# A fourth projection chunk begun at the layer boundary, with its PSUM tile shared with the LayerNorm's mean

## The chip, the cores and the metric

The kernel runs on one core of one Trainium2 chip. The metric is the device time of one execution in microseconds (us); of several runs the median is given. The profile is one execution of the same program taken by the hardware profiler.

Engine names in the profile: PE is TensorE (matrix products), PEld its weight loads, DVE is VectorE, ACT is ScalarE, POOL is GpSimd, SP issues most transfers. SBUF is the on-chip working memory, PSUM the memory into which TensorE writes.

## The reference: what is computed

Two trunk layers run over 640 tokens (128 context tokens and 512 latent tokens) with 1024 features. Cut to what matters here, one layer is:

```python
h = x * (1 + scale) + shift                     # scale, shift from the conditioning
z = h @ w_in + b_in                             # one wide projection, cut into a_q, a_ff, a_fb, ...
...
mixed = einsum('btnd,btnd->btd', gates, proj) @ w_out
y = layer_norm(ALPHA * x + gate * mixed, ln_g, ln_b)   # over the 1024 features of a token
```

The `y` of the first layer is the `x` of the second, so between the layers the kernel must finish the projection by `w_out`, take mean and variance of every token, normalise, form the next layer's `h`, and begin the next `h @ w_in`. Everything is float32; a product is made of three products of a high and a low part in a reduced format (high by high, high by low, low by high).

## The kernel before: tiles, stages and the order of the work

**Layout.** Activations lie with features on the 128 partitions and the 640 tokens along the free axis, as eight tiles of 128 features each. [...]

**Chunks of the projection.** `w_in` is cut into chunks of 128 output columns, named by their use (a_q 0, a_i 0, a_ff 0, d_x 0 and so on). One chunk is one weight tile of 128 by 8 by 128. `take_w` (L163) loads it from memory into a `wraw` tile (three of them), copies it to a high part on ScalarE (L160) and takes the low part on VectorE (L161). High and low parts normally lie in the tiles `whi` and `wlo`, two of each; with `own="s"` they take two of the five large `s` tiles instead. `zmm` (L211) does one chunk for one half: eight steps over the features of h, three products each, accumulated in PSUM (L217).

**PSUM.** It is handed out as two tiles `g` of 512 columns and three tiles `mx` of 1024 columns, and that is all of it. A tile comes free when its last reader is done.

**Who orders the work.** The code is written as one program, and a scheduler of the language turns it into one queue for each engine, in which instructions stay in order: what comes earlier in the program goes first among what is ready by the scheduler's own model of time. It also places all waits between engines. Tiles of a kind (`t`, `e`, `mx`, ...) are handed out in turn.

**Between the layers** (`out_phase`, L1136). For each half, eight chunks of the projection by `w_out` run (L1071), each followed by transposes and statistics of its tokens (L1096, L1098). Then, per half, `out_norm` (L1100) works: it joins the statistics into mean and variance (L1106), takes the inverse root of the variance in small VectorE operations (`rsqrt`, L183), and spreads mean and root over all partitions by transposes on TensorE into one `mx` tile: the mean into columns from 0, the root into columns from 512 (L1112). Then for each of the eight feature tiles: subtract the mean (L1115, VectorE), multiply by the root (L1116, VectorE), form the high part of the next h (L1121, ScalarE) and its full value (L1127 on VectorE, or L1123 on POOL for the first half) in an `e` tile (four of them), take the low part (L1128, VectorE), and keep the scaled y for the next layer's sum (L1129, then a store on SP's queue, L1130).

The norm of the first half runs beside the `w_out` products of the second half. For the norm of the second half there is nothing left of layer 0, so `zopen` (L220) and `zstep` (L232) begin three chunks of the next layer, a_q, a_i and a_g (`FIRST`, L1309): first all their products of the first half, then, after each feature tile of the second half, the three products of that tile for each chunk. The first of the three accumulates in the two `g` tiles, the other two in one `mx` tile each, and the third's weights lie in `s` tiles. The third `mx` tile holds mean and root. The same `zopen` is used at the start of the program (L1186) with the three chunks of layer 0.

In the next layer, `hg_z` (L464) asks for a_q, a_i, a_g and then a_ff; `zchunk` (L237) takes a chunk that was begun early from `self.pre` and only evicts it from PSUM. The chunk after a_ff is d_x.

Of the kernel before, what the change touches and what calls it, by code (L numbers as in the profile page):

```python
# [13 lines left out]
ALU = mybir.AluOpType  # L14
# [3 lines left out]
L = 2  # L18
# [13 lines left out]
def _chunk_cols():  # L32
    names, cols = [], []

    def add(nm, c, i):
        names.append((nm, i))
        cols.append(c)

    def std(nm, i):
        add(nm, np.arange(_OFF[nm] + 128 * i, _OFF[nm] + 128 * i + 128), i)  # L40

    for nm in ("a_q", "a_ff", "a_fb", "a_i", "a_g", "b_q", "b_k", "b_v", "b_g"):
        for i in range(4):
            std(nm, i)
    std("c_qd", 0)
    std("c_qd", 1)
    std("c_kvd", 0)
    k0 = _OFF["c_kpe"]
    add("c_kpe", np.concatenate([np.arange(k0, k0 + 64)] * 2), 0)
    for nm in ("c_g", "d_b", "d_c", "d_x", "d_g"):  # L50
        for i in range(4):
            std(nm, i)
    for i in range(32):
        std("merge", i)
    return {n: i for i, n in enumerate(names)}, np.stack(cols)


CC, COLS = _chunk_cols()
# [29 lines left out]
class Build:  # L88
# [131 lines left out]
    def zopen(self, l, items, own):  # L220

        for nm, i in items:
            n = len(self.pre)
            w = self.take_w(self.I["win"][l, CC[nm, i]], own=own if n == 2 else None)
            if n == 0:
                ps = [self.gps() for _ in range(2)]
            else:
                x = self.mx()
                ps = [x[:, 0:512], x[:, 512:1024]]
            self.pre[nm, i] = w, ps  # L230
# [869 lines left out]
    def out_norm(self, l, p):  # L1100
        nc = self.nc
        a, e = HALVES[p]
        j0, nj, n = a // 128, (e - a) // 128, e - a
        mv = self.sm([128, nj, 2])
        for j in range(nj):
            nc.vector.bn_aggr(mv[:, j, :], self.st[:, j0 + j])  # L1106
        r = self.sm([128, nj])
        self.rsqrt(r, mv[:, :, 1], nj, 1.0, EPS)
        ps = self.mx()
        for src, o in ((mv[:, :, 0], 0), (r, 512)):  # L1110
            for j in range(nj):
                nc.tensor.transpose(ps[:, o + j * 128:o + (j + 1) * 128], src[:, j:j + 1].to_broadcast([128, 128]), self.ident)  # L1112
        for c in range(8):
            y = self.y[c][:, a:e]
            nc.vector.tensor_tensor(y, y, ps[:, 0:n], ALU.subtract)  # L1115
            nc.vector.tensor_tensor(y, y, ps[:, 512:512 + n], ALU.mult)  # L1116
            f = self.e()[:, :n]
            if l + 1 < L:
                for o, x, j in ((0, 128, 0), (128, n, 1)) if p == 0 else ((0, n, 1),):
                    A, B = self.hA[:, c, j:j + 1], self.hB[:, c, j:j + 1]  # L1120
                    nc.scalar.activation(self.h_hi[:, c, a + o:a + x], y[:, o:x], AF.Identity, bias=B, scale=A)  # L1121
                    if p == 0 and F_POOL:
                        nc.gpsimd.tensor_scalar(f[:, o:x], y[:, o:x], A, B, ALU.mult, ALU.add)  # L1123
                    elif p == 1 and F_ACT:
                        nc.scalar.activation(f[:, o:x], y[:, o:x], AF.Identity, bias=B, scale=A)
                    else:
                        nc.vector.tensor_scalar(f[:, o:x], y[:, o:x], A, B, ALU.mult, ALU.add)  # L1127
                nc.vector.tensor_tensor(self.h_lo[:, c, a:e], f, self.h_hi[:, c, a:e].bitcast(F32), ALU.subtract)  # L1128
                nc.scalar.activation(y, y, AF.Identity, bias=self.ag[:, 1, c:c + 1], scale=self.ag[:, 0, c:c + 1])  # L1129
                nc.sync.dma_start(self.ax1[c, :, a:e], y)  # L1130
            else:
                nc.scalar.activation(f, y, AF.Identity, bias=self.vec("lnb", l * 8 + c), scale=self.vec("lng", l * 8 + c))
                nc.sync.dma_start(self.O["yT"][:, c, a:e], f)
            yield c

    def out_phase(self, l):  # L1136
        self.y = [None] * 8
        self.st = self.cp.tile([128, 5, 8, 6], F32, name="st")

        keep = self.bp.tile([128, 5, 8, 128], F32R, name="m")  # L1140
        wk = lambda: self.s([128, 8, 128], F32R)
        own = {2: (keep[:, 0], keep[:, 1]), 3: (keep[:, 2], keep[:, 3]), 4: (keep[:, 4], wk()), 5: (wk(), wk())}
        w = {}
        for p, order in enumerate((range(8), range(7, -1, -1))):
            for n, c in enumerate(order):
                if p == 0 or c < 2:
                    w[c] = self.take_w(self.I["wout"][l, c], own.get(c))
                self.out_chunk(l, c, p, w[c])
                if n:
                    self.out_stats(order[n - 1], p)  # L1150
                if p and n == 1:
                    if l + 1 < L:
                        self.alloc_h()
                    norm = self.out_norm(l, 0)
                if p and n:
                    next(norm, None)
            self.out_stats(order[7], p)
        for _ in norm:
            pass
        if l + 1 < L:  # L1160
            self.zopen(l + 1, FIRST, "s")
            self.zstep((0,), range(8))
            for c in self.out_norm(l, 1):
                self.zstep((1,), (c,))
        else:
            for _ in self.out_norm(l, 1):
                pass
# [141 lines left out]
FIRST = (("a_q", 0), ("a_i", 0), ("a_g", 0))  # L1309
# [139 lines left out]
```

## Time and profile before

| | us |
|---|---|
| median of 3 runs | 2128.25 (2124.88 to 2129.24) |
| the profiled execution | 2125.51 |
| its span, first to last instruction | 2123.4 |
| TensorE busy | 2069.1 |
| VectorE busy | 1366.4 |
| ScalarE busy | 878.8 |
| GpSimd busy | 181.7 |

How to read the profile's lines: in the timeline a line has the start in us from the span's start, the duration in us, the engine, the line of the kernel, the operation, output and inputs by the program's names, sizes, and how many instructions were merged into the line. Behind them, in brackets, stands how long the engine had been idle and what ended that. A PE line's duration includes the time until its result is out, so that the lines of neighbouring products overlap; the spacing of the starts is the time that one takes in a row. In the table of windows, each row gives a stretch, its length, the busy time of PE, PEld, DVE, ACT and POOL with the number of instructions, the granted TensorE clock (1.00 is full), the busy share of the transfer engines and the GB/s moved.

### The profile page before, as it was taken

What the parts mean: (1) busy time and instruction counts of PE and PEld (TensorE: products, weight loads), DVE (VectorE), ACT (ScalarE), POOL (GpSimd) and SP (SyncE); (2) the same over time, 40 slices, a digit from 0 to 9 for tenths busy, and PEclk for the clock granted to TensorE, in tenths of its full rate; (3) what the DMA queues carried; (4) which work ended last, traced back from release to release, by engine and by line L of the source; (5) the groups of instructions that cost most, each with busy time, mean ns of one, the idle gap of its engine ahead of it and who ended that gap; (6) DMA issues with size and microseconds to landing.
All of it is one profiled execution on the core that took longest, in us unless ns stands there. A gap on an engine that the chain in (4) does not pass through costs nothing.

```text
span 2123.4 us, 36900 instructions
## 1 busy us (share of the span) xinstructions
PE 2069.1 (97%) x15114; PEld 2012.1 (95%) x15114; DVE 1366.4 (64%) x2653; ACT 878.8 (41%) x1564; POOL 181.7 (9%) x156
## 2 busy tenths in 40 slices
PE   7999999998999999999999999999999999999997
PEld 4999999997999999999989999999999999999997
DVE  6677676568676567734587776874665546775456
ACT  4333335333445466523353332343343346663332
POOL 0000000121111022200010000020000002231000
PEclk9999999999999999999999999999999999999998
DMA  7222223343334221222432212233222212112241
GB/s 284 74 73 63 66 64 101 115 154 129 125 122 148 69 63 58 66 74 80 141 118 70 71 56 74 61 131 126 85 67 63 67 58 78 60 59 65 75 164 50
DMA packets 79848, 194.64 MB, mean 92 GB/s; under 512 B 9152, under 2 KB 22208, under 8 KB 79680
## 3 DMA queue, kind: packets, MB, share of 16 engines
q1 hardware_dynamic: 76656, 186.10, 27.1%
q10 hardware_dynamic: 3024, 6.20, 0.9%
q8 instruction: 118, 1.93, 0.4%
q14 instruction: 50, 0.41, 0.1%
HBM read 184.73 MB, written 7.54 MB: 91 GB/s over the span
## 4 chain that ended last, share of the span: by engine, by line
PE 87%; DVE 8%; ACT 2%; issue 1%; DMA 1%; POOL 0%; ACTq 0%; SPq 0%; DVEq 0%; POOLq 0%
PE g L217 56%; PE g L208 14%; PE mx L790 2%; PE mx L1005 2%; PE mx L546 2%; PE mx L828 1%; DVE wlo L161 1%; PE mx L208 1%; PE mx L606 1%; PE mx L972 1%; DVE t L161 1%; PE mx L217 1%; PE mx L804 1%; PE mx L583 1%; DVE t L405 1%
## 5 line engine op out<-in xcount | busy, mean ns | idle before, releaser
L217 PE MATMUL g<-h_hi,whi 128*128 128x256 f32 (+1 forms) x2880 | 906.1, 315 | 18.5 <-DVE e L1058 7.4
L217 PE MATMUL g<-h_lo,whi 128*128 128x256 f32 (+1 forms) x2880 | 893.2, 310 | 0.8 <-DVE h_lo L431 0.3
L217 PE MATMUL g<-h_hi,wlo 128*128 128x256 f32 (+1 forms) x2880 | 892.1, 310 | 0.7 <-DVE wlo L161 0.7
L217 PEld LDWEIGHTS g<-h_hi,whi 128*128 128x128 f32 x2880 | 547.9, 190 | 27.1 <-DVE e L1058 8.5
L217 PEld LDWEIGHTS g<-h_lo,whi 128*128 128x128 f32 x2880 | 548.5, 190 | 3.6 <-DVE h_lo L431 1.8
L217 PEld LDWEIGHTS g<-h_hi,wlo 128*128 128x128 f32 x2880 | 548.1, 190 | 1.0 <-DVE wlo L161 1.0
L161 DVE TENSOR_TENSOR wlo<-wraw,whi 128x1024 fp32r<-128x1024 f32 (+1 forms) x258 | 285.7, 1108 | 280.5 <-ACT whi L160 278.5
L160 ACT CAST whi<-wraw 128x1024 fp32r<-128x1024 f32 (+1 forms) x258 | 242.5, 940 | 449.0 <-PE g L217 237.8
L208 PE MATMUL g<-t,whi 128*128 128x256 f32 (+1 forms) x1280 | 283.5, 311 | 0.9 <-ACT e L1043 0.9
L208 PEld LDWEIGHTS g<-t,whi 128*128 128x128 f32 x1280 | 214.2, 189 | 2.7 <-ACT e L1043 1.6
L208 PE MATMUL g<-t,wlo 128*128 128x384 f32 (+1 forms) x640 | 197.8, 309 | 0.0
L407 POOL TENSOR_TENSOR t<-t 128x512 f32<-128x512 f32 x56 | 82.4, 1472 | 1015.8 <-ACT t L406 686.8
L928 POOL TENSOR_SCALAR u<-u,sm 128x320 f32<-128x320 f32 (+2 forms) x80 | 89.9, 1135 | 543.3 <-DVE sm L926 510.5
L208 PEld LDWEIGHTS g<-t,wlo 128*128 128x128 f32 x640 | 121.1, 189 | 0.0
L1043 ACT ACTIVATE e<-g,hbin 128x384 f32<-128x384 f32 (+1 forms) x128 | 66.8, 523 | 105.0 <-PE g L217 102.3
L260 ACT ACTIVATE e<-g,hbin 128x384 f32<-128x384 f32 x76 | 39.9, 525 | 104.0 <-PE g L217 86.7
L261 DVE TENSOR_SCALAR e<-g,vecs 128x384 f32<-128x384 f32 x76 | 41.3, 544 | 51.4 <-ACT e L260 51.1
L476 DVE RECIPROCAL s<-e 128x384 f32<-128x384 f32 (+1 forms) x32 | 68.8, 2149 | 0.7
L405 DVE SCALAR_TENSOR_TENSOR t<-t,cf 128x512 f32<-128x512 f32 x56 | 52.7, 940 | 15.5 <-DMA t<-in_wada 15.4
L853 ACT ACTIVATE t<-mx,sm,rq 128x640 f32<-128x640 f32 (+1 forms) x40 | 31.9, 798 | 63.2 <-DVE sm L850 54.1
L535 ACT COPY t<-s 128x640 f32<-128x640 f32 x56 | 43.4, 779 | 30.3 <-DVE s L560 30.3
L1058 DVE SCALAR_TENSOR_TENSOR e<-e,g 128x384 f32<-128x384 f32 x96 | 46.3, 483 | 13.5 <-PE g L208 12.9
(290 smaller groups left out, 2653.4 us busy)
## 6 DMA issues: line engine op xcount, KB each, us to landing
wraw<-in_win SPq DMA_DIRECT2D x184, 512.0 KB, 3.6
t<-in_wada SPq DMA_DIRECT2D x128, 256.0 KB, 4.3
wraw<-in_wbr SPq DMA_DIRECT2D x64, 256.0 KB, 2.6
wraw<-in_wout SPq DMA_DIRECT2D x20, 512.0 KB, 4.4
s<-in_wada SPq DMA_DIRECT2D x16, 512.0 KB, 6.6
s<-in_nabias SPq DMA_DIRECT2D x8, 640.0 KB, 4.9
m<-in_xT SPq DMA_DIRECT2D x8, 320.0 KB, 7.4
t<-in_xT ACTq DMA_DIRECT2D x8, 320.0 KB, 5.5
```

The source lines that it names most:

```text
L160: nc.scalar.copy(hi, raw)
L161: nc.vector.tensor_tensor(lo, raw, hi.bitcast(F32), ALU.subtract)
L208: nc.tensor.matmul(o, wsl(a, k), xsl(b, k, i), start=(k == 0 and p == 0), stop=(k == nk - 1 and p == 2))
L217: nc.tensor.matmul(ps[:, :e - a], at(u, k), v[:, k, a:e], start=(k == 0 and i == 0), stop=(k == 7 and i == 2))
L405: nc.vector.scalar_tensor_tensor(acc[0], raw[0], c[0], acc[0], ALU.mult, ALU.add)
L407: nc.gpsimd.tensor_tensor(acc[1], acc[1], raw[1], ALU.add)
L476: nc.vector.reciprocal(g, r)
L535: nc.scalar.copy(km.rearrange("p (n u b) -> p n u b", u=2, b=B), ap_of(RK, 0, [[2 * B, np_], [T + B, 2], [1, B]]))
L546: nc.tensor.matmul(ps[r, j * 64:(j + 1) * 64], km[:, o:o + 64], x, start=True, stop=True)
L928: NORM(nc).tensor_scalar(p[e], p[e], sums[:, e:e + 1], None, ALU.mult)
L1043: self.zchunk(l, "merge", n * 8 + c, lambda ps, p, sl: nc.scalar.activation(th[p], ps, AF.Tanh, bias=hb, scale=0.5))
L1058: nc.vector.scalar_tensor_tensor(th[p], th[p], 1.0, ps, ALU.add, ALU.mult)
```

## The change

A fourth chunk, a_ff 0 (the forget gate of the first head), is begun between the layers as well. No PSUM tile is left for it, so it shares one with the norm of the second half:

- It takes the third `mx` tile, called `x3`. Its first half accumulates in columns 512 to 895, its second half in columns 256 to 511. Its weights take two more `s` tiles.
- The norm of the second half spreads its inverse root into columns 0 to 255 of `x3`; ScalarE copies it to an `e` tile in SBUF; then the mean is spread into the same columns 0 to 255 and stays there. The multiplication reads the root from SBUF, the subtraction reads the mean from PSUM.
- The norm of the first half, the norms of the last layer and the start of the program stay as they were.

```diff
@@ zopen
-            w = self.take_w(self.I["win"][l, CC[nm, i]], own=own if n == 2 else None)
+            w = self.take_w(self.I["win"][l, CC[nm, i]], own=own if n >= 2 else None)
             if n == 0:
                 ps = [self.gps() for _ in range(2)]
+            elif n == 3:
+                self.x3 = self.mx()
+                ps = [self.x3[:, 512:1024], self.x3[:, 256:512]]
             else:
                 x = self.mx()
                 ps = [x[:, 0:512], x[:, 512:1024]]
@@ out_norm
-        ps = self.mx()
-        for src, o in ((mv[:, :, 0], 0), (r, 512)):
+        if p and l + 1 < L:
+            ps = self.x3
+            mean, root = ps[:, 0:n], self.e()[:, :n]
+            places = ((r, 0), (mv[:, :, 0], 0))
+        else:
+            ps = self.mx()
+            mean, root = ps[:, 0:n], ps[:, 512:512 + n]
+            places = ((mv[:, :, 0], 0), (r, 512))
+        for src, o in places:
             for j in range(nj):
                 nc.tensor.transpose(ps[:, o + j * 128:o + (j + 1) * 128], src[:, j:j + 1].to_broadcast([128, 128]), self.ident)
+            if src is r and o == 0:
+                nc.scalar.copy(root, ps[:, 0:n])
         for c in range(8):
             y = self.y[c][:, a:e]
-            nc.vector.tensor_tensor(y, y, ps[:, 0:n], ALU.subtract)
-            nc.vector.tensor_tensor(y, y, ps[:, 512:512 + n], ALU.mult)
+            nc.vector.tensor_tensor(y, y, mean, ALU.subtract)
+            nc.vector.tensor_tensor(y, y, root, ALU.mult)
@@ out_phase
-            self.zopen(l + 1, FIRST, "s")
+            self.zopen(l + 1, FIRST + (("a_ff", 0),), "s")
             self.zstep((0,), range(8))
             for c in self.out_norm(l, 1):
                 self.zstep((1,), (c,))
```

## The prediction

> **What bounds the kernel now.** I read the page first (busy shares, chain), then the timeline of each engine where the two layers meet, then the waits.
>
> ```profile
> span 2123.4 us, 36900 instructions
> ...
> PE 2069.1 (97%) x15114; PEld 2012.1 (95%) x15114; DVE 1366.4 (64%) x2653; ACT 878.8 (41%) x1564; POOL 181.7 (9%) x156
> ...
> PE 87%; DVE 8%; ACT 2%; issue 1%; DMA 1%; POOL 0%; ACTq 0%; SPq 0%; DVEq 0%; POOLq 0%
> ```
>
> TensorE is busy for 97% of the span and carries 87% of the chain, so time can only be won where it stands idle. The change touches one such place, the norm of the second half between the layers. TensorE there (start, duration, line):
>
> ```profile
> 1093.13 0.60 PE L1112 MATMUL mx<-ident,sm 128*128 128x128 f32 x4
> 1095.33 0.39 PE L217 MATMUL g<-h_hi,whi 128*128 128x256 f32 x1 [1.60 <-ACT h_hi L1121]
> ...
> 1096.02 0.39 PE L217 MATMUL g<-h_lo,whi 128*128 128x256 f32 x1
> 1096.24 0.28 PE L217 MATMUL g<-h_hi,wlo 128*128 128x256 f32 x1
> 1096.36 0.28 PE L217 MATMUL mx<-h_lo,whi 128*128 128x256 f32 x1
> ...
> 1105.88 0.28 PE L217 MATMUL mx<-h_hi,s 128*128 128x256 f32 x1
> 1106.46 0.44 PE L217 MATMUL g<-h_hi,whi 128*128 128x384 f32 x1 [0.31 <-ACT whi L160]
> ...
> 1107.72 0.44 PE L217 MATMUL g<-h_hi,wlo 128*128 128x384 f32 x1 [0.65 <-DVE wlo L161]
> ...
> 1111.67 0.28 PE L217 MATMUL g<-h_hi,whi 128*128 128x256 f32 x1
> ...
> 1114.54 0.34 PE L217 MATMUL g<-h_hi,whi 128*128 128x384 f32 x1
> ```
>
> A 256-column product takes a slot of 0.12 us (1096.24 to 1096.36). From 1095.33 to 1106.00 (the last one's start plus its slot) run three chunks times eight steps times three products, 72 x 0.12 = 8.64 us of work in 10.67 us, so 2.03 us are lost in the loop, after 1.60 us of waiting for the first h_hi. After the loop 0.31 and 0.65 us go to the weights of the next chunk, which is a_ff. VectorE and ScalarE in the same stretch:
>
> ```profile
> 1087.41 0.16 DVE L195 SCALAR_TENSOR_TENSOR sm<-sm 128x2 f32<-128x2 f32 x1
> 1093.76 0.42 DVE L1115 TENSOR_TENSOR t<-t,mx 128x256 f32<-128x256 f32 x1 [6.20 <-PE mx L1112]
> 1094.22 0.42 DVE L1116 TENSOR_TENSOR t<-t,mx 128x256 f32<-128x256 f32 x1
> ...
> 1095.55 0.42 DVE L1128 TENSOR_TENSOR h_lo<-e,h_hi 128x256 fp32r<-128x256 f32 x1
> ...
> 1104.46 0.42 DVE L1128 TENSOR_TENSOR h_lo<-e,h_hi 128x256 fp32r<-128x256 f32 x1 [0.23 <-ACT h_hi L1121]
> ```
> ```profile
> 1094.68 0.60 ACT L1121 ACTIVATE h_hi<-t,hB,hA 128x256 fp32r<-128x256 f32 x1 [8.29 <-DVE t L1116]
> ...
> 1103.84 0.59 ACT L1121 ACTIVATE h_hi<-t,hB,hA 128x256 fp32r<-128x256 f32 x1
> ...
> 1107.26 0.47 ACT L260 ACTIVATE e<-g,hbin 128x256 f32<-128x256 f32 x1
> ```
>
> VectorE sets the loop's pace: four operations a step, eight steps from 1093.76 to 1104.88, 1.39 us a step against 9 x 0.12 = 1.08 us of TensorE. It runs ahead: it subtracts the mean of step c+1 while TensorE multiplies step c. That running ahead is what the change puts at stake.
>
> **How finely a wait on a PSUM tile is placed.** After the change the mean (columns 0 to 255 of x3) and the second half of a_ff (columns 256 to 511) lie in one tile. The trace shows what such neighbours do to each other:
>
> ```profile
> 1725.58 0.81 DVE L760 TENSOR_TENSOR s<-mx,s 128x640 fp32r<-128x640 f32 x1
> 1726.43 0.27 ACT L762 COPY u<-mx 128x128 f32<-128x128 f32 x1 [1.46 <-DVE s L760]
> ```
> ```profile
> 1728.26 0.38 PE L766 MATMUL mx<-u 128*128 128x128 f32 x2
> ...
> 1728.48 1.28 PE L768 MATMUL mx<-u,t 128*128 128x128 f32 x10
> 1729.80 0.27 ACT L770 COPY u<-mx 128x128 f32<-128x128 f32 x1 [0.35 <-PE mx L768]
> ```
> ```profile
> 2112.78 0.69 PE L1112 MATMUL mx<-ident,sm 128*128 128x128 f32 x2 [2.05 <-DVE sm L195]
> ```
> ```profile
> 2113.51 0.42 DVE L1115 TENSOR_TENSOR t<-t,mx 128x256 f32<-128x256 f32 x1 [0.78 <-PE mx L1112]
> ```
>
> L770 copies columns 640 to 767, which L766 alone wrote by 1728.64. It starts at 1729.80, 0.04 us after the last product of L768, which writes other columns. L762 reads columns that L760 doesn't, and starts 0.04 us after L760 ends. The subtraction at 2113.51 needs only the mean, and starts 0.04 us after the root's transposes into the tile's other 512 columns end. So an access to a tile waits for every earlier access of another engine to that tile (at the least, to that stretch of 512 columns). In the changed loop, L1115 of step c+1 reads the tile that a_ff's products of step c wrote just before in program order: it must wait for them, and VectorE can no longer run ahead.
>
> **The sum, part by part.** Times within a step count from the start of its subtraction.
>
> The loop. Subtraction to multiplication 0.46 (1093.76 to 1094.22); to h_hi another 0.46 (1094.68); h_hi 0.60 and 0.03 more to h_lo (1103.84 + 0.59 = 1104.43 to 1104.46), so h_lo runs from 1.55 to 1.97. The multiplication now reads the root from SBUF; L1128, two SBUF operands of the same size, takes the same 0.42, so nothing changes there. TensorE starts the four products with h_hi 0.05 after h_hi, at 1.57; the first occupies 0.22 (1096.02 to 1096.24), three more 0.12 each, free at 2.15, after h_lo is there (1.97 + 0.05). The remaining eight start at 2.15, the last at 2.99; it ends 0.28 later, and 0.03 after that (1093.73 to 1093.76) the next subtraction may start: 3.30 us a step. In the rows above, products that become ready together go in the order of the chunks (g, mx, mx), so I put a_ff last. Eight steps: 7 x 3.30 + 2.99 + 0.12 = 26.21 us from the first subtraction to a free TensorE. Before it was 1106.00 - 1093.76 = 12.24. Term: +13.97. Queued behind the waiting subtraction are L1116, L1127 and L1128 of its own step, and all of ScalarE, TensorE and the store of the row wait on these. Nothing fills in: other chunks' accumulators in g and mx are complete but unread, since their evictions take e tiles, which are handed out after those of the eight steps.
>
> a_ff's second half leaves its old place, where it took 1114.54 - 1111.67 = 2.87: -2.87. Its first half (24 products) moves ahead of the transposes and leaves the later place: 0. The root was ready at 1087.57 and waits for TensorE until 1093.13 anyway.
>
> The root. Before, four transposes to subtraction: 1093.76 - 1093.13 = 0.63. Now two (0.38), 0.04 until ScalarE's copy (0.47, by L260 of the same size), 0.05, two transposes (0.38), 0.03: 1.35. Term: +0.7. The mean's transposes can't go first, since both use the same columns.
>
> After the loop the next chunk is d_x, whose weights need the tile that a_q's last product frees, as a_ff's did. Nine products instead of six cover it, but ScalarE's last y and the wait chain come as late; I take 0, between -0.4 (three products of 0.12) and +0.4.
>
> ```profile
> 1069.69 1.22 DVE L161 TENSOR_TENSOR s<-wraw,s 128x1024 fp32r<-128x1024 f32 x1
> ```
> ```profile
> 1075.00:1090.00 15.00, 14.92 (x99) 14.40 (x98) 11.86 (x35) 8.10 (x13) 4.24 (x7) 1.00 0.43 138
> ```
>
> The split of a_ff's weights, 1.22 us of VectorE, comes before the norm instead of after it. VectorE is busy for 11.86 of 15 us there (fourth number), so there is room: 0, with 1.2 as the other end, if it delays h of the first half. Its transfer needs no new place: SP issues it fourth as before. Setting the first layer up uses three chunks as before.
>
> The clock. TensorE will now stand mostly idle around the copy, 1.35 + 1.57 us with four short transposes in them. Rows of the windows (the last but two is the granted clock), and products at the low clock:
>
> ```profile
> 18.20:20.20 2.00, 0.00 (x0) 0.00 (x0) 1.96 (x8) 1.05 (x3) 0.00 (x0) 1.00 1.05 412
> 20.30:23.00 2.70, 2.66 (x11) 1.11 (x11) 2.64 (x6) 2.70 (x6) 0.00 (x0) 1.00 1.03 405
> 51.70:53.50 1.80, 0.00 (x0) 0.00 (x0) 1.39 (x11) 1.20 (x3) 0.00 (x0) 1.00 0.01 5
> 54.00:57.00 3.00, 2.67 (x10) 2.16 (x10) 2.91 (x10) 0.79 (x3) 0.00 (x0) 0.50 0.00 0
> ```
> ```profile
> 55.93 0.41 PE L217 MATMUL g<-h_lo,whi 128*128 128x256 f32 x1
> 56.14 0.41 PE L217 MATMUL g<-h_hi,wlo 128*128 128x256 f32 x1
> ```
>
> One pause of 2 us left the clock at 1.00, another was followed by 3 us at 0.50, with slots of 0.21. A step at half clock: four products from 1.57 free TensorE at about 2.5, eight more start until 2.5 + 7 x 0.21 = 3.97, and 0.41 + 0.03 later the step ends: 4.41, or 1.1 more. Nearer to the pause of nearly 3 us lies the second case; I take one step: +1.1, between 0 and eight steps.
>
> [...]
>
> Sum: 13.97 - 2.87 + 0.7 + 1.1 = +12.9. The profiled execution took 2125.51 us (2123.4 of span and 2.1 around it) and would take 2138.4. It lies 2.74 below the median of the runs, 2128.25, from which I forecast 2141.2 (+0.6%).
>
> **Rivals.** *Waits by address.* If neighbouring columns don't wait, VectorE runs ahead as before. TensorE then sets the pace: 1.57 + 96 x 0.12 = 13.1, with some 0.4 of losses 13.5, against 12.24: +1.3 - 2.87 + 0.7 - 0.3 (weights) = -1.2, time 2127.1, not slower; if the copy of the root hid too and every loss went (1.60 + 2.03 + 0.96 = 4.6), 2123.7. For it speaks that VectorE has the data; against it all three pairs above.
>
> [...]
>
> *a_ff first.* If TensorE's order puts a_ff's products ahead of the other chunks' in each step, the subtraction is released after two of the eight: 2.15 + 0.12 + 0.28 + 0.03 = 2.58 a step, 7 x 0.72 = 5.0 less, 2136.2. Against it: the order in the rows is g, then mx.
>
> *Half clock throughout.* With 12 x 0.12 = 1.44 us of products in 3.30, the clock may stay at half: 7 x 1.1 more, 2148.9. Against it: at half clock the products fill 12 x 0.21 of 4.41, 57%, and the row of 54 to 57 shows the clock coming back after 3 us of such work.
>
> **How the numbers follow.** About 0.2% (4.3 us) is what a measurement of this kernel can tell from no change. Forecast 0.78, half clock 0.06, a_ff first 0.06, by address 0.10. The range runs from a_ff first with a spread of 1.2 (2135.0) to the forecast with 1.2 for the split and five more steps at half clock (2148.0). It leaves out the case by address, half clock throughout and a tail of 0.04. Slower are all cases but the one by address: 0.90; of that, 0.08 lies within 0.2%, and 0.02 is for every loss gone.
>
> **What would show it.** In the changed profile L1115 should wait for L217 into mx in seven steps, for about 1.3 us each (from h_lo's end at 1.97 to 3.30), the loop should last 26 us, VectorE and TensorE take turns, and ScalarE's copy stand between two pairs of transposes. If L1115 follows L1116 of the step before without a wait, the first rival holds and the forecast falls; if the steps last 2.6, the second; if the windows of the loop show 0.50 throughout, the third.

## The result and the profile after

| | before, us | after, us |
|---|---|---|
| median (runs), first series | 2127.94 (6) | 2142.26 (6: 2138.11 to 2151.99) |
| ratio after / before, first series | | 1.0074 (95%: 1.0061 to 1.0087) |
| median (runs), second series | 2128.17 (27) | 2140.17 (5: 2138.65 to 2140.55) |
| ratio after / before, second series | | 1.0053 (1.0040 to 1.0065) |
| the profiled execution | 2125.51 | 2138.11 |
| its span | 2123.4 | 2136.3 |

The kernel became slower by 0.5 to 0.7%: 14.3 us between the medians of the first series, 12.0 between those of the second, and the two intervals overlap. One run of before in the first series took 2256.12 us, counts as a slow one and is left out of the ratio (the median of the other five is 2127.64). The page of the changed kernel begins so, and its largest group of products (times of the group, mean ns of one, then the idle time before it) reads:

```profile
span 2136.3 us, 36899 instructions
...
PE 2069.1 (97%) x15114; PEld 2012.0 (94%) x15114; DVE 1368.1 (64%) x2653; ACT 879.6 (41%) x1565; POOL 182.2 (9%) x156
...
L217 PE MATMUL g<-h_hi,whi 128*128 128x384 f32 (+1 forms) x2864 | 901.6, 315 | 28.1 <-ACT h_hi L1134 12.9
```

TensorE's busy time is the same to a tenth, 2069.1 us, and the span is 12.9 us longer: all that was added is idleness. In after, 12.9 us of idleness in all were ended by the high part of h (L1134 now, L1121 before). That both figures are 12.9 is chance: 1.60 of this wait stood in before too, so 11.3 us of it are new. TensorE in the stage where the layers meet (start, duration, line; the bracket is the idle time before and what ended it):

```profile
1099.17 0.38 PE L1123 MATMUL mx<-ident,sm 128*128 128x128 f32 x2
1100.01 0.43 PE L1123 MATMUL mx<-ident,sm 128*128 128x128 f32 x2 [0.46 <-ACT e L1125]
1102.12 0.39 PE L217 MATMUL g<-h_hi,whi 128*128 128x256 f32 x1 [1.68 <-ACT h_hi L1134]
...
1103.42 0.28 PE L217 MATMUL mx<-h_lo,s 128*128 128x256 f32 x1
1103.54 0.28 PE L217 MATMUL mx<-h_hi,s 128*128 128x256 f32 x1
1105.42 0.39 PE L217 MATMUL g<-h_hi,whi 128*128 128x256 f32 x1 [1.61 <-ACT h_hi L1134]
```

In L217's lines the products of 384 columns are those of the first half of the tokens (0 to 383), those of 256 columns of the second (384 to 639). The order is: the root's two transposes, ScalarE's copy, the mean's two transposes; then twelve products, a pause of 1.6 us, twelve products, and so on eight times. Before, such a pause stood only ahead of the first step (1.60). What VectorE did in the same stretch:

```profile
1100.55 0.42 DVE L1128 TENSOR_TENSOR t<-t,mx 128x256 f32<-128x256 f32 x1 [10.03 <-PE mx L1123]
1101.01 0.42 DVE L1129 TENSOR_TENSOR t<-t,e 128x256 f32<-128x256 f32 x1
1101.47 0.41 DVE L1140 TENSOR_SCALAR e<-t,hA,hB 128x256 f32<-128x256 f32 x1
1102.10 0.43 DVE L1141 TENSOR_TENSOR h_lo<-e,h_hi 128x256 fp32r<-128x256 f32 x1 [0.22 <-ACT h_hi L1134]
1103.86 0.42 DVE L1128 TENSOR_TENSOR t<-t,mx 128x256 f32<-128x256 f32 x1 [1.33 <-PE mx L217]
...
1107.16 0.42 DVE L1128 TENSOR_TENSOR t<-t,mx 128x256 f32<-128x256 f32 x1 [1.33 <-PE mx L217]
```

The subtraction (L1115 before, L1128 now) waits 1.33 us for a product into an `mx` tile. It starts at 1103.86; the last of the twelve products began at 1103.54 and has its result out 0.28 later, at 1103.82. The waits of the stretch in one view say that it happens in all seven later steps (total us, times, longest):

```profile
DVE t L1128 <- PE mx L1123: 10.0, 1, 10.0
DVE t L1128 <- PE mx L217: 9.3, 7, 1.3
```

So VectorE prepares a step, TensorE multiplies it, and each stands still while the other works. The windows show what the clock did meanwhile (the last but two is the granted clock):

```profile
1099.00:1102.00 3.00, 0.98 (x6) 0.46 (x5) 1.26 (x3) 0.91 (x2) 0.00 (x0) 1.00 0.00 0
1102.00:1105.00 3.00, 1.70 (x12) 1.50 (x12) 1.50 (x4) 0.90 (x3) 0.00 (x0) 1.00 0.13 44
1105.00:1108.00 3.00, 1.70 (x12) 1.50 (x12) 1.42 (x4) 0.97 (x2) 0.00 (x0) 1.00 0.15 46
...
1117.00:1120.00 3.00, 1.40 (x12) 1.37 (x12) 1.68 (x4) 1.20 (x2) 0.00 (x0) 1.00 0.06 18
```

It stayed at 1.00 in every such row from 1096 to 1129. The stage ends so:

```profile
1081.38 0.42 PE L217 MATMUL g<-h_hi,whi 128*128 128x384 f32 x1
...
1126.65 0.28 PE L217 MATMUL mx<-h_hi,s 128*128 128x256 f32 x1
1127.23 0.44 PE L217 MATMUL g<-h_hi,whi 128*128 128x384 f32 x1 [0.30 <-ACT whi L160]
...
1128.49 0.44 PE L217 MATMUL g<-h_hi,wlo 128*128 128x384 f32 x1 [0.64 <-DVE wlo L161]
```

The first of these lines is the first early product of a_q, the last three the end of the loop and the beginning of d_x. In before the same first product stands here:

```profile
1079.80 0.42 PE L217 MATMUL g<-h_hi,whi 128*128 128x384 f32 x1
```

From a_q's first product to d_x's first product went 1114.54 - 1079.80 = 34.74 us before and 1127.23 - 1081.38 = 45.85 after: 11.11 more. The 0.64 that d_x then waits for its low weights was paid inside this stretch by a_ff before (0.65), so the stage costs 11.75 us more. Of the 12.9 us between the spans another 1.58 (1081.38 - 1079.80) were there before the stage began, and 0.4 came back after it. The 1.58 are no work of the change: 1.61 us stood already at a pair of transposes some 53 us earlier (1026.93 before, 1028.54 after). The profiled executions scatter by as much there: before and the three kernels with three chunks below that change nothing ahead of it have their first a_q product between 1079.14 and 1082.12.

### The profile page after: what moved, and what is told of

Same layout as the page of the kernel before. It is cut to its first block, busy times and chain, and to the rows that moved or that the text cites. A ratio compares the mean times of both kernels' runs of the same rounds, so it can differ in the third digit from the quotient of the medians.

```text
span 2136.3 us, 36899 instructions
## 1 busy us (share of the span) xinstructions
PE 2069.1 (97%) x15114; PEld 2012.0 (94%) x15114; DVE 1368.1 (64%) x2653; ACT 879.6 (41%) x1565; POOL 182.2 (9%) x156
## 4 chain that ended last, share of the span: by engine, by line
PE 87%; DVE 8%; ACT 2%; DMA 2%; issue 1%; POOL 0%; ACTq 0%; SPq 0%; DVEq 0%; POOLq 0%
PE g L217 56%; PE g L208 13%; PE mx L793 2%; PE mx L1008 2%; PE mx L549 2%; PE mx L217 1%; PE mx L831 1%; DVE wlo L161 1%; PE mx L208 1%; PE mx L609 1%; PE mx L975 1%; DVE t L161 1%; PE mx L807 1%; PE mx L586 1%; DVE e L660 1%
## 5 line engine op out<-in xcount | busy, mean ns | idle before, releaser
L217 PE MATMUL g<-h_hi,whi 128*128 128x384 f32 (+1 forms) x2864 | 901.6, 315 | 28.1 <-ACT h_hi L1134 12.9
L217 PE MATMUL g<-h_lo,whi 128*128 128x384 f32 (+1 forms) x2864 | 887.7, 310 | 1.0 <-DVE h_lo L434 0.7
L217 PE MATMUL g<-h_hi,wlo 128*128 128x384 f32 (+1 forms) x2864 | 887.3, 310 | 0.6 <-DVE wlo L161 0.6
L217 PEld LDWEIGHTS g<-h_hi,whi 128*128 128x128 f32 x2864 | 544.8, 190 | 38.0 <-ACT h_hi L1134 14.6
L217 PEld LDWEIGHTS g<-h_lo,whi 128*128 128x128 f32 x2864 | 545.7, 191 | 2.4 <-DVE h_lo L434 1.6
L217 PEld LDWEIGHTS g<-h_hi,wlo 128*128 128x128 f32 x2864 | 545.1, 190 | 1.0 <-DVE wlo L161 1.0
```

Source lines behind the costliest of these rows:

```text
L217: nc.tensor.matmul(ps[:, :e - a], at(u, k), v[:, k, a:e], start=(k == 0 and i == 0), stop=(k == 7 and i == 2))
```

## The experiments

The theory: the subtraction waits because the mean lies in a tile into which the products of the step before were written, whatever columns; this stops VectorE from running ahead, and that is all of the loss. The rivals: the wait goes by columns or by stretches of 512 columns, and the time goes elsewhere (the detour of the root, four chunks instead of three, the clock). All kernels compute the whole result.

**The mean out of the shared tile.** The changed kernel, and ScalarE also copies the mean to an `e` tile, so that nothing in the loop reads the shared tile:

```diff
+        if p and l + 1 < L:
+            mean = self.e()[:, :n]
+            nc.scalar.copy(mean, ps[:, 0:n])
         for c in range(8):
```

> The changed kernel, but the mean too is copied from PSUM to an e tile by ScalarE, so that the subtraction no longer reads the tile into which a_ff's products go. Theory (the subtraction waits for the tile): the eight steps run ahead again and last about 13.5 us instead of 26.2; with 0.4 us for the second copy the time comes to 2127 to 2128 us, within 0.1% of the kernel before. Rival (the fourth chunk's 24 extra products in the loop, or the detour of the root, cost the time): the loop stays near 26 us and the time near 2142 us.

Measured: 2127.93 us (11 runs) against 2127.23 of before (15): 1.0001 (0.9992 to 1.0010). The loss is gone with the fourth chunk, the shared tile and the detour of the root all in place, and a further copy added. VectorE in that kernel (L1131 is the subtraction, L1132 the multiplication):

```profile
1100.79 0.76 DVE L1131 TENSOR_TENSOR t<-t,e 128x256 f32<-128x256 f32 x2 [10.34 <-ACT e L1128]
...
1103.46 0.76 DVE L1131 TENSOR_TENSOR t<-t,e 128x256 f32<-128x256 f32 x2
...
1106.11 0.76 DVE L1131 TENSOR_TENSOR t<-t,e 128x256 f32<-128x256 f32 x2
```

Two subtractions at a time, without a wait, every 2.65 us: 1.33 us a step in place of 3.30. But why is it not faster than before, with fuller steps? TensorE and the clock there:

```profile
1099.92 0.43 PE L1123 MATMUL mx<-ident,sm 128*128 128x128 f32 x2 [0.46 <-ACT e L1125]
1102.58 0.39 PE L217 MATMUL g<-h_hi,whi 128*128 128x256 f32 x1 [2.23 <-ACT h_hi L1137]
...
1103.84 0.41 PE L217 MATMUL mx<-h_hi,wlo 128*128 128x256 f32 x1
1104.05 0.42 PE L217 MATMUL mx<-h_lo,s 128*128 128x256 f32 x1
```
```profile
1100.00:1103.00 3.00, 0.78 (x5) 0.53 (x6) 2.21 (x7) 1.45 (x4) 0.00 (x0) 1.00 0.00 0
1103.00:1106.00 3.00, 3.00 (x17) 2.85 (x16) 3.00 (x10) 2.42 (x6) 0.00 (x0) 0.59 0.28 91
1106.00:1109.00 3.00, 3.00 (x23) 3.00 (x23) 3.00 (x10) 2.42 (x6) 0.00 (x0) 0.84 0.27 89
```

Ahead of the loop TensorE stands for 0.46 and 2.23 us (before: 1.60), and about 15 products then run in slots of 0.21 (1103.84 to 1104.05) instead of 0.12, some 1.4 us. What the fourth chunk fills in the loop, the longer road to the first h takes away: from a_q's first product to d_x's first product go 1115.99 - 1081.25 = 34.74 us, the same as in before.

**a_ff first in each step.** In the second half the chunks are gone through backwards, so that six products lie behind the last one into the shared tile that had none behind it:

```diff
     def zstep(self, ps, ks):
-        for w, b in self.pre.values():
+        for w, b in reversed(list(self.pre.values())) if len(self.pre) == 4 and ps == (1,) else self.pre.values():
```

> The changed kernel, but in each of the eight steps a_ff's products stand first in the program, ahead of those of a_q, a_i and a_g. Theory: the subtraction waits only for the products into its own tile, so a step shrinks by the six products behind them (6 x 0.12 = 0.72 us) from 3.30 to about 2.58 us, and the time by about 5 us to 2137 us. Rival (the subtraction waits for all of TensorE's work of the step, or the steps are set by VectorE and ScalarE alone): steps stay at 3.30 us and the time at 2142 us.

Measured: 2134.38 us (4 runs), 1.0037 (1.0023 to 1.0051). The subtractions of this kernel:

```profile
1102.78 0.42 DVE L1128 TENSOR_TENSOR t<-t,mx 128x256 f32<-128x256 f32 x1 [0.62 <-PE mx L217]
...
1105.37 0.42 DVE L1128 TENSOR_TENSOR t<-t,mx 128x256 f32<-128x256 f32 x1 [0.62 <-PE mx L217]
```

A step takes 2.59 us and the wait 0.62: by so much less than 3.30 and 1.33 as six slots of 0.12 are worth (0.72). The wait ends with the last product into the shared tile and not with the step. The forecast of the step holds. The time lies 2.6 us below the 2137 us that were expected; from the changed kernel's second series (2140.17) it fell by 5.8 us, where seven steps of 0.72 make 5.0.

**The shared tile without the fourth chunk, and how wide a wait is.** Two kernels made from the one before, with its three chunks. The norm of the second half takes mean and root as in the change, and the second half of a_g (the third chunk) lies in the norm's tile: once in columns 256 to 511 beside the mean, once in columns 512 to 767.

```diff
+            elif n == 2 and l:
+                x, self.x3 = self.mx(), self.mx()
+                ps = [x[:, 0:512], self.x3[:, 256:512]]
```
```diff
+                ps = [x[:, 0:512], self.x3[:, 512:768]]
```

Columns 256 to 511:

> The kernel before with its three chunks, but a_g's second half accumulates in the norm's tile, in columns 256 to 511 beside the mean; the root goes to SBUF as in the change. No fourth chunk. Theory (the wait alone makes the loss): steps of about 2.94 us (three chunks' nine products instead of twelve), loop 23.3 us against 12.2, root +0.75, time about 2140 us. Rival (the fourth chunk makes the loss): time as before, 2128 to 2129 us.

Columns 512 to 767:

> As e3_same_bank, but a_g's second half lies in columns 512 to 767 of the norm's tile, in the other 512 columns than the mean. Theory A (a wait covers the whole tile): steps of 2.94 us and about 2140 us, the same as e3_same_bank. Theory B (a wait covers 512 columns): no wait, loop near 12 to 13 us and 2128 to 2129 us.

Measured: 2144.64 us (4 runs), 1.0085 (1.0064 to 1.0105), and 2145.39 (4 runs), 1.0085 (1.0070 to 1.0100). The subtractions of the first (L1127 there), then of the second:

```profile
1097.04 0.42 DVE L1127 TENSOR_TENSOR t<-t,mx 128x256 f32<-128x256 f32 x1 [1.06 <-PE mx L217]
...
1100.94 0.42 DVE L1127 TENSOR_TENSOR t<-t,mx 128x256 f32<-128x256 f32 x1 [1.92 <-PE mx L217]
```
```profile
1097.15 0.42 DVE L1127 TENSOR_TENSOR t<-t,mx 128x256 f32<-128x256 f32 x1 [1.06 <-PE mx L217]
...
1101.04 0.42 DVE L1127 TENSOR_TENSOR t<-t,mx 128x256 f32<-128x256 f32 x1 [1.92 <-PE mx L217]
```

The same waits to the hundredth, 1.06 and 1.92 us, in both places of the products in the tile: in these two kernels it is the tile that is waited for, not columns and not a stretch of 512 (theory A). And the loss comes with the sharing alone, without a fourth chunk. Its size was missed: with nine products a step it should have been below the change's, and it is above. Windows of the first of the two say why:

```profile
1094.00:1097.00 3.00, 1.43 (x9) 1.19 (x9) 1.68 (x4) 1.20 (x2) 0.00 (x0) 1.00 0.00 0
1097.00:1100.00 3.00, 1.39 (x7) 1.39 (x7) 1.69 (x4) 1.20 (x2) 0.00 (x0) 0.64 0.13 43
1100.00:1103.00 3.00, 1.40 (x7) 1.10 (x6) 1.68 (x4) 1.12 (x2) 0.00 (x0) 0.50 0.13 44
...
1118.00:1121.00 3.00, 2.29 (x9) 1.99 (x9) 0.99 (x3) 0.62 (x2) 0.00 (x0) 0.50 0.13 44
```

The first step took 3.04 us (the subtractions at 1094.00 and 1097.04), at full clock; in the second the clock falls (0.64 in the row from 1097, 0.50 from 1100 on), the nine products go in slots of 0.21, and a step takes 3.89. So here happened what the prediction's third rival described for the change.

**The changed kernel once more**, to see whether its runs fall into two groups, with and without the low clock:

> The changed kernel once more, for its spread. Theory: with steps of 3.30 us at the full clock the time is 2139 to 2141 us (11.8 us above before by the sum without the clock); runs in which the clock halves in the loop (steps of 4.4 us) come to 2148 to 2152 us with a mean granted clock near 0.98, so that the times fall into two groups by their clock. Rival (the clock plays no part in the spread): times of one group, without relation to the clock.

Measured: 2140.17 us (5 runs, 2138.65 to 2140.55), 1.0053 (1.0040 to 1.0065), the mean clock 0.988 to 0.990 in all five. Of the two groups of the theory, only the one at full clock appeared in this series. Its profile repeats the first:

```profile
1101.46 0.42 DVE L1128 TENSOR_TENSOR t<-t,mx 128x256 f32<-128x256 f32 x1 [10.04 <-PE mx L1123]
1104.75 0.42 DVE L1128 TENSOR_TENSOR t<-t,mx 128x256 f32<-128x256 f32 x1 [1.32 <-PE mx L217]
```

In the first series one run of six stood apart, 2151.99 us at a mean clock of 0.981 where the other five had 0.988 to 0.990. A mean lower by 0.009 over 2150 us is 0.009 x 2150 / 0.5 = 39 us at half clock, and the whole loop at half clock would last about 8 x 4.41 = 35. That fits a loop at half clock throughout, but no trace of that run exists: it is an estimate from the mean clocks and the forecast step of 4.41.

**Cover instead of sharing.** TensorE's pause while the norm becomes ready can be filled with products that need no norm. From the changed kernel: mean and root go into the shared tile side by side, one copy brings both to SBUF (a `t` tile), and the first half of a_ff comes behind the transposes instead of ahead of them:

```diff
+        if p and l + 1 < L:
+            nc.scalar.copy(both[:, 0:2 * n], ps[:, 0:2 * n])
+            w, b = self.pre["a_ff", 0]
+            self.zmm(b[0], w, 0, range(8))
```

> Four chunks; mean and root go to SBUF in one copy of ScalarE, and a_ff's first half (24 products, 4.15 us) stands behind the transposes in the program, so that it runs while the root is copied and the first h of the second half is made. Theory: TensorE no longer pauses for 2.9 us around the copy, the clock stays at 1.00, and the loop is set by TensorE (96 x 0.12 = 11.5 us): about 3 us below before, 2124.5 us. Rival (a copy out of the tile makes the products into its other columns wait as well, and the pauses stay): the same as before within 0.1%.

Measured: 2124.07 us (11 runs) against 2128.17 (27): 0.9979 (0.9971 to 0.9988). The cover begins late, since its products go into the tile that is being copied:

```profile
1098.82 0.44 PE L217 MATMUL mx<-h_hi,s 128*128 128x384 f32 x1 [0.68 <-ACT t L1126]
...
1115.98 0.44 PE L217 MATMUL g<-h_hi,wlo 128*128 128x384 f32 x1 [0.64 <-DVE wlo L161]
```

The pause at the copy, 0.68 us, is a wait for the whole tile once more, now on TensorE: the products write other columns than the copy reads, and the first starts at 1098.82, 0.06 us after the copy's end (1098.18 + 0.58). So the rival's mechanism is there, but it costs 0.68 us and not the gain. From there on TensorE is without a wait until d_x's low weights.

**Cover with three chunks.** From the kernel before, without a fourth chunk and without sharing: only the first half of a_g comes behind the transposes of the second half's norm.

```diff
+        if p and l + 1 < L:
+            w, b = self.pre["a_g", 0]
+            self.zmm(b[0], w, 0, range(8))
         for c in range(8):
...
-            self.zopen(l + 1, FIRST, "s")
+            self.zopen(l + 1, FIRST[:2], "s")
             self.zstep((0,), range(8))
+            self.zopen(l + 1, FIRST[2:], "s")
```

> The kernel before with its three chunks; only a_g's first half (24 products) moves behind the transposes of the second half's norm. Theory: the 1.60 us of waiting for the first h_hi and the loop's losses of 2.03 us lie beside these products: 3 to 3.5 us below before, 2124 us, without a fourth chunk. Rival (VectorE's eight steps of 1.39 us end the loop as late as before): the same as before.

Measured: 2123.50 us (11 runs), 0.9984 (0.9974 to 0.9993). TensorE there:

```profile
1091.46 0.60 PE L1112 MATMUL mx<-ident,sm 128*128 128x128 f32 x4
1091.81 0.42 PE L217 MATMUL mx<-h_hi,s 128*128 128x384 f32 x1
...
1105.18 0.44 PE L217 MATMUL g<-h_hi,whi 128*128 128x384 f32 x1 [0.30 <-ACT whi L160]
```

From the transposes to the next chunk go 13.72 us, with no wait in between but the 0.30 at the end. Before, it was 1106.46 - 1093.13 = 13.33, and the 24 products that now lie inside (24 x 0.173 = 4.15) came ahead of it: 17.48 for the same work, 3.76 more. VectorE now gets ahead while a_g's products run, so the loop's pauses go as well as the first. The gain needs no fourth chunk.

**The weights after the loop.** The same, and the weights of a_i also in tiles of their own, so that `whi` and `wlo` are free early for the chunk after the loop:

```diff
-            w = self.take_w(self.I["win"][l, CC[nm, i]], own=own if n == 2 else None)
+            w = self.take_w(self.I["win"][l, CC[nm, i]], own=own if n == 2 else "t" if n == 1 and l else None)
```

> As e6_three_cover, and a_i's weights take t tiles instead of whi and wlo, so that the next chunk's weights are split before the loop ends. Theory: the 0.31 and 0.65 us of waiting for weights after the loop go too: 1 to 1.5 us below e6_three_cover, 2123 us. Rival (the t tiles come free too late, or the waiting moves to another weight): no difference to e6_three_cover.

Measured: 2123.42 us (11 runs), 0.9977 (0.9969 to 0.9986), not to be told from the kernel without it. TensorE there:

```profile
1077.55 0.44 PE L1096 MATMUL mx<-ident,t 128*128 128x128 f32 x2 [0.61 <-DVE t L1088]
...
1085.48 0.44 PE L1096 MATMUL mx<-ident,t 128*128 128x128 f32 x2 [0.45 <-DVE t L1088]
...
1093.56 0.60 PE L1112 MATMUL mx<-ident,sm 128*128 128x128 f32 x4
...
1106.82 0.34 PE L217 MATMUL g<-h_hi,whi 128*128 128x384 f32 x1
```

The two waits for weights after the loop are gone (13.26 us from the transposes to the next chunk, and no bracket on it), but transposes ahead of the norm now wait 0.61 and 0.45 us for VectorE, which they did not in the kernel without it. These 1.06 us give back what the two waits were worth (13.72 + 0.64 - 13.26 = 1.10), so the rival holds: the waiting moved.

## Why the prediction was right, point by point

- **The loop, +13.97.** Forecast 26.21 us from the first subtraction to a free TensorE; measured 1126.65 + 0.12 - 1100.55 = 26.22. The step 3.30, measured 3.30 (1103.86 to 1107.16); the wait "about 1.3 us each" in seven steps, measured 1.33 in seven. That the shared tile is its cause was argued from neighbours in the trace of before; the kernel with the mean in SBUF and the two kernels with a_g in the norm's tile show it.
- **Order within a step.** Put last, a_ff costs 3.30; put first, 2.59 (2.58 in that rival). Its time came to 2134.4 where the rival said 2136.2.
- **The root, +0.7.** Measured 1100.55 - 1099.17 = 1.38 against 0.63, +0.75. The copy took 0.37 us instead of the 0.47 taken for it; the second pair of transposes (0.43 instead of 0.38) and the way from it to the subtraction (0.11 instead of 0.03) made up for that.
- **a_ff's halves, -2.87 and 0; the end, 0.** The stage as a whole came to +11.75 against 13.97 - 2.87 + 0.7 = +11.8. The weights' waits behind the loop appear with d_x as they did with a_ff (0.30 and 0.64), and the earlier split of a_ff's weights has left no cost that the profile shows: from the transposes at 1026.93 and 1028.54 to a_q's first product it is 52.87 us before and 52.84 after.
- **The clock, +1.1: the mis-sized term.** One step at half clock was forecast; both profiles of the changed kernel show 0. Without the term the sum is 2128.25 + 13.97 - 2.87 + 0.7 = 2140.1, and the second series measured 2140.17. The first lies 1.1 above the forecast (2142.26 against 2141.2), with one run of 2151.99. That it came so near with a term that the profiles don't show is luck: the two series differ by more than the term. So the term is nothing in both profiles and perhaps the whole of "half clock throughout" in the one run. One step, the value between, was in no trace.
- **The rival of half clock throughout.** The argument against it doesn't hold. The row of 54 to 57 has TensorE busy for 2.67 of 3.00 us, 89% and not 57%, and it is all at 0.50; the clock was 0.82 from 57 to 58 and 1.00 from 58 to 61. And with a_g in columns 256 to 511 of the norm's tile nine products in slots of 0.21 filled 1.89 of the 3.00 us from 1118 to 1121, 63%, and the clock was still 0.50 there and in the two rows behind it. The profiled executions of the changed kernel escaped this rival because their clock didn't fall in the loop (1.00 in its rows, steps of 3.30 us from the first to the last), not because it came back.
- **The rival by address, 2127.1.** Its condition did not hold. With the mean taken out of the tile VectorE does run ahead and the time is 2127.93, near this rival's number, but partly by other terms: the loop lasts 1115.89 - 1100.79 = 15.10 us against the 13.5 of its working, with some 1.4 for the half clock, and a second copy stands ahead of it.

What stays open is what makes the clock fall. Ahead of the loop the changed kernel and the one with a_g in columns 512 to 767 have the same pauses (0.46 and 1.68 us), so the pause alone doesn't decide here. The first step has twelve products in 3.30 us in the one and nine in 3.03 in the other; after it the clock was 1.00 in two profiles of two, and 0.50 in the profiles of both kernels with nine. No run varied the number of products alone, so the cause was not shown.

## What to carry to other kernels

Before putting an accumulator beside a broadcast operand in one PSUM tile, ask whether a loop's reader runs ahead of the loop's writer: here the wait covered the tile in columns 256 to 511 and 512 to 767 alike (1.06 and 1.92 us in both), and it turned 1.39 us a step into 3.30. Accesses to neighbouring columns elsewhere in the same trace show this beforehand (they began 0.04 us after the others' end), and the price follows from laying the step's operations end to end. A small operand that a loop reads is better held in SBUF (with the mean there a step took 1.33 us in place of 3.30), and a latency is better covered by holding back work that doesn't depend on it (0.9984 and 0.9979 of the time here) than by doing that work ahead of it.

## What the runs showed of the hardware

The granted clock is read here from rows of 3.00 us. With the mean in SBUF TensorE is busy for 0.78 us of the row from 1100, at 1.00; the next two rows have 0.59 and 0.84, and from 1109 on it is 1.00. In the two kernels with a_g in the norm's tile the rows from 1094 and 1097 have 1.00 and 0.64 (columns 256 to 511) and 1.00 and 0.69 (columns 512 to 767); then it is 0.50 up to 1127 and up to 1124. The first of these rows in the kernel with columns 512 to 767, and behind them a row of the changed kernel (the number behind the length is TensorE's busy time):

```profile
1094.00:1097.00 3.00, 1.32 (x10) 1.19 (x9) 1.68 (x4) 1.20 (x2) 0.00 (x0) 1.00 0.00 0
1097.00:1100.00 3.00, 1.40 (x8) 1.28 (x7) 1.68 (x4) 1.20 (x2) 0.00 (x0) 0.69 0.13 44
1100.00:1103.00 3.00, 1.40 (x7) 1.10 (x7) 1.67 (x4) 1.01 (x2) 0.00 (x0) 0.50 0.13 44
```
```profile
1120.00:1123.00 3.00, 1.40 (x12) 1.19 (x12) 1.68 (x4) 1.20 (x2) 0.00 (x0) 1.00 0.13 44
```

What makes the clock fall was not shown. TensorE's busy time in such a row doesn't tell the cases apart: 1.43 and 1.32 us in the two rows from 1094 were followed by 0.64 and 0.69, while 1.40 in the changed kernel was followed by 1.00. Nor do the pauses: the longest ahead of the falls is 2.23 us with the mean in SBUF and 1.68 with a_g in the norm's tile, and the changed kernel had one of 1.68 without a fall.

At half clock, nine products in slots of 0.21 fill 1.9 of 3.89 us, 49%, and with a_g in the norm's tile the rows from 1100 to 1124 are at 0.50. At full clock, twelve in slots of 0.12 fill 1.44 of 3.30 us, 44%, and in the changed kernel the rows from 1096 to 1129 are at 1.00. A loop that was about half idle thus kept either clock here.
